# Residual added in the thirteenth pair, first pair copied to the sum; first products of the last four experts, then their second products

## The chip, the cores and the metric

The kernel runs on one core of a Trainium2 chip. The metric is the device time of one execution in microseconds (us), the median of several runs. TensorE is called PE here, VectorE DVE, ScalarE ACT, GpSimd POOL, SyncE SP; PEld is the loading of PE's stationary operand. A matrix product writes PSUM, which has eight banks.

## The reference

One decoder layer: attention over 256 tokens of width 2048, a residual and a layer norm, then a mixture of 32 experts in 4 groups, and another residual and layer norm. The change lies in the second half:

```python
def hierarchical_moe(x, w_grp, b_grp, w_rt, b_rt, w_gate, w_up, w_down):
    ...                       # one group per token, in it the two best experts: comb
    for g in range(N_GROUPS):
        h = jax.nn.silu(jnp.einsum('td,edf->tef', xt, w_gate[g])) * jnp.einsum('td,edf->tef', xt, w_up[g])
        h = h * comb[:, g, :, None]
        y = y + jnp.einsum('tef,efd->td', h, w_down[g])
    return y.reshape(B, S, D)

def reference(...):
        ...
        x = layer_norm(DEEPNORM_ALPHA * x + y, mix_ln_g[i], mix_ln_b[i])
        y = hierarchical_moe(x, ...)
        x = layer_norm(DEEPNORM_ALPHA * x + y, ffn_ln_g[i], ffn_ln_b[i])
```

Each expert has 12 MiB of weights in float32: gate and up (2048 x 512 each) and down (512 x 2048).

## The kernel before

The first 420 us are attention and the first norm. Then the 32 experts follow in 16 pairs. The tokens chosen by an expert (up to 64 in the first pass) are gathered by products with one-hot matrices, so that a pair fills the 128 rows of PE's output.

For a pair `p` the order on PE is written out by hand (`manual_schedule` for PE and SP; DVE, ACT and POOL run in program order too from the first norm on):

- **First products** (`gate_up`, L518): for each of the two experts (`side`) four blocks `j` of gate and up weights, 1 MiB each. After a block, `used` frees its two slots.
- Between the blocks of the first expert, `rest(j)` scatters a quarter of the previous pair's result back to its tokens (`scatter`, L540 and L541, tile `cb`), and DVE adds it to the sum `acc` (L548).
- `slots_of` (tile `m`) after the first expert, `hidden` after each: ACT's SiLU (L522) and DVE's multiplication (L523) give `hs`.
- The **gather** for the next pair (`pg`, L485, copied to `xg` by DVE L492 and ACT L494), eight steps through two PSUM banks that `mb()` hands out in turn; after the sixth the hidden values are transposed (`hp`, L528; `ht`, L530).
- **Second products** (`y`, L686): four steps `k` of down weights, two blocks of 1 MiB each; then ACT and DVE split the first two quarters of `y` in two parts (L534, L535, `ys_all`) for the scatter.

`residual(n)` sets the sum up, quarter by quarter in the blocks of the first expert of pair 1: PE spreads a part of the first norm's gain and shift over the 128 rows (`rows_of`, L555, tiles `g` and `b`, through `mb()`), DVE multiplies the normalised input by the gain into `acc` (L565) and adds the shift (L567). Pair 14 has eight more such broadcasts (tile `r`) for the last norm's gain and shift (copied by ACT, L667).

After pair 10 all four `rest` run in one piece, and then `further_passes`, a loop whose number of passes is read at run time (L591).

The last pair's down weights come in five column blocks (`wl`, 1 MiB each for the first three of each expert; the last two half as wide), so that `last_down` (L720), `last_add` and the sums of the last norm work block by block.

All weights come through the SP queue (L384) into a ring of slots of 1 MiB, in the order of the list `pieces`; a load is issued when a slot is free. The first 21 blocks lie ready when the experts begin.

Of the kernel before, what the change touches and what calls it, by code (L numbers as in the profile page):

```python
# [17 lines left out]
P = 128  # L18
# [11 lines left out]
LOOP_AFTER = 10  # L30
LOOP_SLOTS = 4
# [23 lines left out]
def hybrid_kernel(ctx: ExitStack, tc: tile.TileContext, x, w_qkv, w_o, ln1_g, ln1_b, w_grp, b_grp,  # L55
# [310 lines left out]
    for pr in range(NP):  # L366
# [5 lines left out]
        if pr < NP - 1:  # L372
            for k in range(4):
                pieces += [(("d", e, k), [wd_v[e, k]]) for e in (2 * pr, 2 * pr + 1)]
# [168 lines left out]
    def add_rows(name, n, ot, ys, banks, rows=P):  # L543
        for tt in range(NT):
            cb = bank(banks[tt], [P, 512], f"cb{name}_{n}_{tt}")
            scatter(cb, ot, ys, tt, rows=rows)
            t = acc[tt][:, n * 512:(n + 1) * 512]
            nc.vector.tensor_add(t, t, cb)  # L548
# [10 lines left out]
    def residual(n):  # L559

        cs = slice(n * 512, (n + 1) * 512)
        g_ = rows_of(0, n, mb(), f"g1_{n}")
        b_ = rows_of(1, n, mb(), f"b1_{n}")
        for tt in range(NT):
            nc.vector.scalar_tensor_tensor(acc[tt][:, cs].rearrange("p (a c) -> p a c", c=4), xn[tt][:, n].rearrange("p c a -> p a c"),  # L565
                                           ALPHA, g_.rearrange("p (a c) -> p a c", c=4), op0=ALU.mult, op1=ALU.mult)
# [78 lines left out]
    for p in range(NP):  # L645
# [3 lines left out]
        for side in range(2):  # L649
            e = 2 * p + side  # L650
            for j in range(4):
                gate_up(gu[side], side, lambda c: xg[:, c, side], j, held["g", e, j], held["u", e, j])
                used(("g", e, j), ("u", e, j), keep=keep)
                if p == side == 0 and j < 2:
                    for c2 in (2 * j + 4, 2 * j + 5):
                        gather(c2, xg, o2, 0)
                if p == side == 0 and j == 1:
                    gatef = gates()
                    count_passes()
                if p == 1 and side == 0:  # L660
                    residual(j)
                if side == 0 and rest is not None:
                    rest(j)
                if p == NP - 2:
                    vec = 2 + j % 2
                    n = 2 * side + j // 2
                    nc.scalar.copy(held["v", vec, 0][:, n * 512:(n + 1) * 512], rows_of(vec, n, mb(), f"r2_{n}_{vec}"))  # L667
# [4 lines left out]
        if p + 1 < NP:  # L672
            o2 = o2_next
            xg = slot(S_XG, [P, NCH, 2, CAP], f"xg{p + 1}")
            for c2 in range(8):
                gather(c2, xg, o2, p + 1)
                if c2 == 5:
                    ht = transpose_hidden(hs, p)
        else:
            ht = transpose_hidden(hs, p)  # L680
            break
        y = [bank(yb[n], [P, 512], f"y{p}_{n}") for n in range(4)]
        for k in range(4):
# [4 lines left out]
            used(("d", 2 * p, k), ("d", 2 * p + 1, k), keep=keep)  # L688
# [11 lines left out]
        if p == LOOP_AFTER:  # L700
# [4 lines left out]
            advance()  # L705

# [124 lines left out]
```

## Time and profile before

| what | value |
|---|---|
| median of 3 runs | 1395.65 us (1393.35 to 1395.83) |
| the profiled execution | 1393.51 us, its span 1391.8 us |
| busy share of the span | PE 96%, DVE 33%, ACT 24%, POOL 1% |
| granted clock of PE, mean | 0.989 |
| read from memory | 472.20 MB |
| chain of waits, by engine | PE 60%, DMA 28%, DVE 3%, ACT 2%, issue 6% |

The span goes from the first to the last instruction of the profiled execution; the rest of its time lies around it. The chain of waits is followed back from the last instruction to whatever released each step. PE counts as busy also where it runs at half clock.

### The profile page before, as it was taken

The numbers are of one execution on the slowest core, as the hardware profiler recorded it, in microseconds if no ns is written. First come the engines' busy times: TensorE is split into PE (matmuls) and PEld (weight loads), VectorE is DVE, ScalarE is ACT, GpSimd is POOL, SyncE is SP. The second block draws the span as 40 slices with busy tenths as digits, with TensorE's granted clock in tenths as the row PEclk, the third lists the DMA queues.
The fourth block names the chain that finished last, engine by engine and source line by source line (L and its number), as shares of the span: only waits on it lengthen the run. The fifth ranks groups of instructions, "written<-read, shape, count | busy, mean of one in ns | idle before, by whom it ended". The sixth has DMA issues, their size and how long they took to land.

```text
span 1391.8 us, 17936 instructions
## 1 busy us (share of the span) xinstructions
PE 1339.9 (96%) x7537; PEld 802.0 (58%) x7537; DVE 452.5 (33%) x797; ACT 332.1 (24%) x567; POOL 16.3 (1%) x39
## 2 busy tenths in 40 slices
PE   9999999999999999999999999999998999999994
PEld 8999898988895454434344344453434344344432
DVE  5454645455443151221222212212123021212116
ACT  4454535345334101101011011110101011011103
POOL 0000100000000000000000000000000000000002
PEclk9999999999999999999999999999999999999997
DMA  9745455576559889999999999999999999999993
GB/s 341 243 152 182 151 175 189 180 258 238 174 208 371 357 336 381 420 420 418 420 420 419 420 418 420 420 418 420 419 420 420 417 419 420 419 420 421 419 396 105
DMA packets 103016, 475.52 MB, mean 342 GB/s; under 512 B 12756, under 2 KB 18964, under 8 KB 54804
## 3 DMA queue, kind: packets, MB, share of 16 engines
q1 hardware_dynamic: 102932, 474.33, 86.1%
q8 instruction: 61, 1.00, 0.3%
q14 instruction: 23, 0.19, 0.0%
HBM read 472.20 MB, written 2.10 MB: 341 GB/s over the span
## 4 chain that ended last, share of the span: by engine, by line
PE 60%; DMA 28%; issue 6%; DVE 3%; ACT 2%; POOL 0%; SPq 0%; DVEq 0%; POOLq 0%; ACTq 0%
DMA wu<-in_moe_w_up_dram 20%; PE gu L518 18%; PE y L686 9%; DMA wd<-in_moe_w_down_dram 7%; PE pg L485 5%; PE pj L163 5%; PE pj L161 5%; PE pj L162 5%; PE wo L163 2%; PE wo L161 2%; PE wo L162 2%; PE cb L540 1%; PE cb L541 1%; PE y L720 1%; ACT xg L494 1%
## 5 line engine op out<-in xcount | busy, mean ns | idle before, releaser
L518 PE MATMUL gu<-wu,xg 128*64 128x512 f32 x1024 | 461.6, 600 | 7.5 <-DMA wu<-in_moe_w_up_dram 7.5
L518 PE MATMUL gu<-wg,xg 128*64 128x512 f32 x1024 | 461.1, 600 | 4.9 <-PEq L591 4.9
L518 PEld LDWEIGHTS gu<-wg,xg 128*64 128x64 f32 x1024 | 135.1, 138 | 225.7 <-issue 216.7
L686 PE MATMUL y<-wd,ht 128*64 128x512 f32 x960 | 209.3, 594 | 0.0
L518 PEld LDWEIGHTS gu<-wu,xg 128*64 128x64 f32 x1024 | 135.0, 138 | 61.7 <-issue 44.9
L161 PE MATMUL pj<-xh,ws 128*128 128x256 f32 x512 | 146.4, 286 | 0.8 <-ACT ws L151 0.8
L152 DVE TENSOR_TENSOR ws<-w,ws 128x1024 fp32r<-128x1024 f32 x88 | 107.9, 1226 | 120.7 <-ACT ws L151 120.7
L163 PE MATMUL pj<-xh,ws 128*128 128x256 f32 x512 | 146.0, 285 | 0.6 <-DVE ws L152 0.6
L162 PE MATMUL pj<-xl,ws 128*128 128x256 f32 x512 | 146.1, 286 | 0.0
L686 PEld LDWEIGHTS y<-wd,ht 128*64 128x64 f32 x960 | 67.6, 137 | 130.3 <-issue 127.6
L485 PE MATMUL pg<-o,xn 128*128 128x128 f32 x1024 | 131.5, 283 | 10.9 <-ACT xg L494 6.4
L485 PEld LDWEIGHTS pg<-o,xn 128*128 128x128 f32 x1024 | 120.3, 191 | 32.5 <-issue 13.0
L548 DVE TENSOR_TENSOR acc<-acc,cb 128x512 f32<-128x512 f32 x120 | 77.2, 684 | 181.6 <-PE cb L541 181.6
L151 ACT CAST ws<-w 128x1024 fp32r<-128x1024 f32 x88 | 92.4, 1050 | 133.6 <-PE pj L163 130.9
L534 ACT CAST ys_all<-y 128x512 fp32r<-128x512 f32 x60 | 35.1, 585 | 302.7 <-PE y L686 161.8
L535 DVE TENSOR_TENSOR ys_all<-y,ys_all 128x512 fp32r<-128x512 f32 x60 | 41.3, 688 | 184.0 <-ACT ys_all L534 181.8
L163 PEld LDWEIGHTS pj<-xh,ws 128*128 128x128 f32 x512 | 98.1, 192 | 1.3 <-DVE ws L152 1.2
L161 PEld LDWEIGHTS pj<-xh,ws 128*128 128x128 f32 x512 | 98.1, 192 | 1.2 <-ACT ws L151 1.0
L162 PEld LDWEIGHTS pj<-xl,ws 128*128 128x128 f32 x512 | 98.1, 192 | 0.1
L523 DVE SCALAR_TENSOR_TENSOR hs<-hs,gs,gu 64x512 f32<-64x512 f32 x32 | 23.9, 747 | 225.4 <-ACT hs L522 224.2
L494 ACT ACTIVATE xg<-pg,gbp 128x128 f32<-128x128 f32 x128 | 51.6, 453 | 97.7 <-PE pg L485 97.7
L492 DVE TENSOR_SCALAR xg<-pg,gbp 128x128 f32<-128x128 f32 x128 | 46.6, 406 | 85.4 <-PE pg L485 85.2
(197 smaller groups left out, 1222.4 us busy)
## 6 DMA issues: line engine op xcount, KB each, us to landing
wg<-in_moe_w_gate_dram SPq DMA_DIRECT2D x128, 1024.0 KB, 19.9
wu<-in_moe_w_up_dram SPq DMA_DIRECT2D x128, 1024.0 KB, 19.9
wd<-in_moe_w_down_dram SPq DMA_DIRECT2D x120, 1024.0 KB, 19.9
w<-in_attn_w_qkv_dram SPq DMA_DIRECT2D x44, 1024.0 KB, 5.2
wow<-in_attn_w_o_dram SPq DMA_DIRECT2D x16, 1024.0 KB, 5.1
wl<-in_moe_w_down_dram SPq DMA_DIRECT2D x6, 1024.0 KB, 17.2
wfirst<-in_attn_w_qkv_dram SPq DMA_DIRECT2D x3, 1024.0 KB, 11.0
xs<-in_x_dram SPq DMA_DIRECT2D x8, 256.0 KB, 8.3
```

Of the source, the lines that this page charges most:

```text
L151: nc.scalar.copy(t[:, 0, c], src[:, c])
L152: nc.vector.tensor_sub(t[:, 1, c], src[:, c], t[:, 0, c].bitcast(F32))
L161: nc.tensor.matmul(dst, ah, bh, start=start, stop=False, **kw)
L162: nc.tensor.matmul(dst, ah, bl, start=False, stop=False, **kw)
L163: nc.tensor.matmul(dst, al, bh, start=False, stop=stop, **kw)
L485: nc.tensor.matmul(pg[:, cc], xn[tt][:, n, c, :], o2[:, tt].rearrange("p e s -> p (e s)"), start=tt == 0, stop=tt == 1)
L492: nc.vector.tensor_scalar(to, pg[:, cc], g_, b_, op0=ALU.mult, op1=ALU.add)
L494: nc.scalar.activation(to, pg[:, cc], AF.Identity, scale=g_, bias=b_)
L518: nc.tensor.matmul(gu[to], xg(4 * j + c), w[:, c, :], start=st, stop=sp, skip_group_check=True)
L535: nc.vector.tensor_sub(ys[0:rows, 1, 0:width], y[0:rows, 0:width], ys[0:rows, 0, 0:width].bitcast(F32))
L548: nc.vector.tensor_add(t, t, cb)
L686: nc.tensor.matmul(y[n][sides[side]], ht[:, k, sides[side]], held["d", 2 * p + side, k][:, n * 512:(n + 1) * 512], start=k == 0, stop=k == ...
```

## The change

The residual moves from the first expert of pair 1 to the second expert of pair 12 (`RES_AT`, counted from 0), one quarter after each of its blocks. Since the sum is no longer set up first, pair 0's scatter is copied to `acc` instead of added. The residual is added to what the sum holds by then: the gain is spread once for each half of the tokens, multiplied in its PSUM bank by the normalised input, and added; then the shift is spread and added to both halves.

The last two pairs go in another order: first products of pair 14, first products of pair 15, second products of pair 14, its scatters in one piece, then the last products of pair 15. The list of loads follows. The banks and slots of the last stage change places accordingly.

```diff
+RES_AT = 12
...
-        if pr < NP - 1:
-            for k in range(4):
-                pieces += [(("d", e, k), [wd_v[e, k]]) for e in (2 * pr, 2 * pr + 1)]
+        if pr == NP - 1:
+            pr -= 1
+        elif pr == NP - 2:
+            continue
+        for k in range(4):
+            pieces += [(("d", e, k), [wd_v[e, k]]) for e in (2 * pr, 2 * pr + 1)]
...
-            nc.vector.tensor_add(t, t, cb)
+            if name == 0:
+                nc.vector.tensor_copy(t, cb)
+            else:
+                nc.vector.tensor_add(t, t, cb)
...
     def residual(n):
 
         cs = slice(n * 512, (n + 1) * 512)
-        g_ = rows_of(0, n, mb(), f"g1_{n}")
+        for tt in range(NT):
+            g_ = rows_of(0, n, mb(), f"g1_{n}_{tt}")
+            g4 = g_.rearrange("p (a c) -> p a c", c=4)
+            nc.vector.scalar_tensor_tensor(g4, xn[tt][:, n].rearrange("p c a -> p a c"), ALPHA, g4, op0=ALU.mult, op1=ALU.mult)
+            nc.vector.tensor_add(acc[tt][:, cs], acc[tt][:, cs], g_)
         b_ = rows_of(1, n, mb(), f"b1_{n}")
         for tt in range(NT):
-            nc.vector.scalar_tensor_tensor(acc[tt][:, cs].rearrange("p (a c) -> p a c", c=4), xn[tt][:, n].rearrange("p c a -> p a c"),
-                                           ALPHA, g_.rearrange("p (a c) -> p a c", c=4), op0=ALU.mult, op1=ALU.mult)
             nc.vector.tensor_add(acc[tt][:, cs], acc[tt][:, cs], b_)
...
+    def between(p, i):
...
+        if i < 4 and rest is not None:
+            rest(i)
+        if p == RES_AT and i >= 4:
+            residual(i - 4)
+        if p == NP - 2:
+            n, vec = divmod(i, 2)
+            nc.scalar.copy(held["v", 2 + vec, 0][:, n * 512:(n + 1) * 512], rows_of(2 + vec, n, mb(), f"r2_{n}_{vec}"))
+
+    for p in range(NP - 1):
+        hs, ot, o2 = first_products(p)
+        xg = slot(S_XG, [P, NCH, 2, CAP], f"xg{p + 1}")
+        for c2 in range(8):
+            gather(c2, xg, o2, p + 1)
+            if c2 == 5:
+                ht = transpose_hidden(hs, p)
+        if p == NP - 2:
+            rest = None
+            hs, last_ot, _ = first_products(p + 1)
+        y = second_products(p, ht)
...
+    p, ot = NP - 1, last_ot
+    ht = transpose_hidden(hs, p)
+    for n in range(4):
+        rest(n)
...
-    last_y, last_cob, lys = Rot([4, 5]), Rot([6, 7, 0, 1]), []
+    last_y, last_cob, lys = Rot([0, 1]), Rot([4, 5, 6, 7]), []
...
-        ys = slot((*S_XN, S_XG, S_YS)[n % 4], [P, 2, 512], f"ys{p}_{n}", F32R)
+        ys = slot((*S_XN, S_XG)[n % 3], [P, 2, 512], f"ys{p}_{n}", F32R)
```

`first_products`, `second_products` and `between` hold what stood in the loop's body.

On PE, this is the end of the first block of pair 1 before the change (`gu_0` is the first expert's product, `g_0` and `b_0` the broadcasts, `cb` the scatter of pair 0):

```order
3054 L518 MATMUL gu_0_4285<-wg_0_4039,xg_4168 64x512
3055 L518 MATMUL gu_0_4285<-wu_0_4087,xg_4168 64x512
3056 L555 MATMUL g_0_4300<-gb_896,ident 128x128 x4
3057 L555 MATMUL b_0_4305<-gb_896,ident 128x128 x4
3058 L540 MATMUL cb_0_0_4314<-ys_all,ot_4111 128x512
```

The broadcasts `g` and `b` are gone from there. In the changed kernel PE has them in pair 12, after each block of the second expert (`gu_1`); this is the end of the first and the beginning of the second block:

```order
4827 L522 MATMUL gu_1_7522<-wg_0_7395,xg_7401 64x512
4828 L522 MATMUL gu_1_7522<-wu_0_7397,xg_7401 64x512
4829 L562 MATMUL g_0_0_7635<-gb_896,ident 128x128 x4
4830 L562 MATMUL g_0_1_7642<-gb_896,ident 128x128 x4
4831 L562 MATMUL b_0_7649<-gb_896,ident 128x128 x4
4832 L522 MATMUL gu_1_7522<-wg_1_7477,xg_7401 64x512
```

Three broadcasts stand in a row there. On DVE, the last quarter of the residual in pair 12 of the changed kernel (`hs` is the second expert's hidden values, `xg` the gathered rows of pair 13):

```order
628 L572 SCALAR_TENSOR_TENSOR g_3_0_7734<-xn_3898,g_3_0_7734 128x512
629 L573 TENSOR_TENSOR acc_4279<-acc_4279,g_3_0_7734 128x512
630 L572 SCALAR_TENSOR_TENSOR g_3_1_7741<-xn_3899,g_3_1_7741 128x512
631 L573 TENSOR_TENSOR acc_4280<-acc_4280,g_3_1_7741 128x512
632 L576 TENSOR_TENSOR acc_4279<-acc_4279,b_3_7748 128x512
633 L576 TENSOR_TENSOR acc_4280<-acc_4280,b_3_7748 128x512
634 L527 SCALAR_TENSOR_TENSOR hs_7523<-hs_7523,gs_7617,gu_1_7522 64x512
635 L496 TENSOR_SCALAR xg_7757<-pg_0_7758,gbp 128x128 x2
```

Before, `hs` of pair 12 followed the first expert's `hs` at once. At the end, the transposition of pair 15's hidden values stood on PE right behind its first products:

```order
5308 L518 MATMUL gu_1_8440<-wg_3_8431,xg_8319 64x512
5309 L518 MATMUL gu_1_8440<-wu_3_8433,xg_8319 64x512
5310 L528 MATMUL hp_8574<-ident,hs_8441 128x128 x4
5311 L720 MATMUL y_0_8581<-wl_0_8450,ht_8579 64x512
5312 L720 MATMUL y_0_8581<-wl_1_8452,ht_8579 64x512
```

Now it stands behind pair 14's second products, and pair 14's sixteen scatter products stand between it and the last products:

```order
5296 L677 MATMUL y_3_8529<-wd_3_8458,ht_8395 64x512
5297 L677 MATMUL y_3_8529<-wd_3_8460,ht_8395 64x512
5298 L532 MATMUL hp_8566<-ident,hs_8413 128x128 x4
5299 L544 MATMUL cb_0_0_8573<-ys_all,ot_8266 128x512
5300 L545 MATMUL cb_0_0_8573<-ys_all,ot_8266 128x512
```

## Rows read from the trace of the kernel before

**Rows 1.** From the page: the rate of all transfers in 40 equal slices of the span (34.8 us each), and one group of DVE instructions (line, engine, operation, out<-in, count | busy us, mean ns | idle before and its end).

```profile
GB/s 341 243 152 182 151 175 189 180 258 238 174 208 371 357 336 381 420 420 418 420 420 419 420 418 420 420 418 420 419 420 420 417 419 420 419 420 421 419 396 105
...
L548 DVE TENSOR_TENSOR acc<-acc,cb 128x512 f32<-128x512 f32 x120 | 77.2, 684 | 181.6 <-PE cb L541 181.6
```

**Rows 2.** The chain of waits from 400 us to the end, in order of time: start us, length us, what.

```profile
469.83 13.88 PE y L686 x64
...
512.40 15.14 PE gu L518 x64
...
536.80 13.88 PE y L686 x64
...
569.93 13.93 PE gu L518 x64
583.89 0.60 ACT hs L522
...
586.06 4.12 PE pg L485 x32
...
593.12 13.88 PE y L686 x64
...
649.43 13.88 PE y L686 x64
...
780.04 19.87 DMA wu<-in_moe_w_up_dram
...
1044.68 0.60 ACT hs L522
...
1235.05 13.88 PE y L686 x64
...
1253.50 1.08 PE r L555 x8
...
1315.10 3.43 PE gu L518 x16
1319.66 3.58 PE gu L518 x16
```

**Rows 3.** What PE waited for from 1080 to 1180 us (total us, times, longest), and from PE's timeline the second products of pair 12.

```profile
PE gu L518 <- PEq L591: 4.9, 1, 4.9
PE pg L485 <- ACT xg L494: 0.8, 2, 0.4
PE pg L485 <- DVE xg L492: 0.5, 2, 0.3
...
1176.19 13.95 PE L686 MATMUL y<-wd,ht 128*64 128x512 f32 x64
```

**Rows 4.** Stretches of the span: length, then busy us (and count) of PE, PEld, DVE, ACT and POOL, PE's granted clock, the DMA share, GB/s.

```profile
480.00:560.00 80.00, 78.42 (x406) 37.36 (x404) 29.62 (x48) 9.59 (x20) 0.00 (x0) 0.98 0.90 363
560.00:780.00 220.00, 217.39 (x1107) 97.09 (x1108) 48.71 (x101) 29.56 (x63) 0.00 (x0) 1.00 1.01 419
```

**Rows 5.** Timelines of PE (first two rows and the last) and of DVE in pair 1: start us, length us, engine, line, operation, out<-in, shape, count [idle before and what ended it].

```profile
486.55 0.59 PE L518 MATMUL gu<-wg,xg 128*64 128x512 f32 x1
487.07 1.15 PE L555 MATMUL g<-gb,ident 16*128 16x128 f32 x8
...
488.26 1.03 DVE L565 SCALAR_TENSOR_TENSOR acc<-xn,g 128x512 f32<-128x512 f32 x1 [4.91 <-PE g L555]
489.40 0.69 DVE L567 TENSOR_TENSOR acc<-acc,b 128x512 f32<-128x512 f32 x1
490.00 1.06 DVE L565 SCALAR_TENSOR_TENSOR acc<-xn,g 128x512 f32<-128x512 f32 x1
...
510.06 1.02 DVE L565 SCALAR_TENSOR_TENSOR acc<-xn,g 128x512 f32<-128x512 f32 x1
...
511.23 0.52 PE L503 MATMUL m<-ident,o 128*128 128x128 f32 x2 [0.92 <-DVE acc L565]
```

**Rows 6.** Short stretches, with the columns of rows 4: behind the last quarter of the residual in pair 1, and among the scatters of pair 10.

```profile
512.00:513.00 1.00, 1.00 (x4) 0.61 (x6) 1.00 (x3) 0.54 (x2) 0.00 (x0) 0.50 0.93 393
...
1072.00:1074.00 2.00, 1.49 (x5) 0.79 (x6) 1.71 (x4) 0.00 (x0) 0.00 (x0) 1.00 1.03 426
```

**Rows 7.** PE's timeline at the scatters of pair 10, with the columns of rows 5.

```profile
1067.73 0.50 PE L540 MATMUL cb<-ys_all,ot 128*128 128x512 f32 x1
...
1072.33 0.47 PE L540 MATMUL cb<-ys_all,ot 128*128 128x512 f32 x1 [1.15 <-DVE ys_all L535]
...
1074.14 0.40 PE L541 MATMUL cb<-ys_all,ot 128*128 128x512 f32 x1
```

**Rows 8.** PE's timeline at the last products, with the columns of rows 5.

```profile
1349.70 0.66 PE L528 MATMUL hp<-ident,hs 128*128 128x128 f32 x4 [1.48 <-DVE hs L523]
1351.04 8.78 PE L720 MATMUL y<-wl,ht 128*64 128x512 f32 x32 [0.68 <-ACT ht L530]
...
1360.87 3.65 PE L720 MATMUL y<-wl,ht 128*64 128x512 f32 x16
...
1368.58 1.95 PE L720 MATMUL y<-wl,ht 128*64 128x256 f32 x16
```

**Rows 9.** What reads or loads the tile `wl`: the issues of its loads (duration ns min/median/max, first and last start us), and the us from issue to landing.

```profile
L384 SPq DMA_DIRECT2D wl<-in_moe_w_down_dram x10: 373/2508/9307, 1324.8 to 1354.7; - x10
...
DMA to landing us min/median/max: 9.6/13.6/20.3
```

More of the change, by code (lines that the diff above doesn't have):

```diff
@@ L644, in hybrid_kernel, with first_products @@
     gatef, ys_all, acc, rest = None, None, None, None
-    for p in range(NP):
+    def first_products(p):
         keep = LOOP_SLOTS if p == LOOP_AFTER else 0
@@ L653, in hybrid_kernel @@
                 used(("g", e, j), ("u", e, j), keep=keep)
[L654 to L667, printed above, removed]
+                between(p, 4 * side + j)
             if side == 0:
@@ L671, in hybrid_kernel, with second_products @@
             hidden(gu[side], side, gs, hs)
[L672 to L681, printed above, removed]
+        return hs, ot, o2_next
+    def second_products(p, ht):
         y = [bank(yb[n], [P, 512], f"y{p}_{n}") for n in range(4)]
@@ L687, in hybrid_kernel @@
                                      start=k == 0, stop=k == 3, skip_group_check=True)
-            used(("d", 2 * p, k), ("d", 2 * p + 1, k), keep=keep)
+            used(("d", 2 * p, k), ("d", 2 * p + 1, k), keep=LOOP_SLOTS if p == LOOP_AFTER else 0)
+        return y
+    def between(p, i):
+        nonlocal gatef
+        if p == 0 and i < 2:
+            for c2 in (2 * i + 4, 2 * i + 5):
+                gather(c2, xg, o2, 0)
+        if p == 0 and i == 1:
+            gatef = gates()
+            count_passes()
+        if i < 4 and rest is not None:
[16 more added lines that the diff above has]
+        y = second_products(p, ht)
         if p == 0:
```

## The prediction, made before the changed kernel was run

> **What bounds the kernel now.** I read the page first, then the chain of waits from 400 us on. The loads move 417 to 421 GB/s from the seventeenth slice almost to the end, and TensorE (PE) is busy 96% of the span, so a busy share decides nothing [rows 1]. A pair of experts loads 24 blocks of 1 MiB, 25.2 MB, which at 420 GB/s takes 59.9 us. PE alone needs 56.3 us for a pair: that is the distance between the second products of pairs 1, 2 and 3 (536.80, 593.12, 649.43) [rows 2]. The two are close, and the chain shows who holds when:
>
> - Until 780 us PE holds. Pair 1, with the residual in it, takes 66.97 us (469.83 to 536.80), 10.66 more than the others [rows 2].
> - From 780 us the loads hold, up to the first products of pair 10, which end at 1044.68 on a late load [rows 2].
> - Pair 10 runs its four scatters in one piece and then reaches the branch of the further passes, where PE stands 4.9 us. Between 1080 and 1180 us PE waits for no load at all, only 1.3 us inside gathers [rows 3]. The loads have caught up with it in pair 13 alone: second products start at 1176.19 and 1235.05, 58.86 us apart, so PE waited 2.55 us there [rows 2, 3].
> - From there to the final block the chain is PE again, and pair 14 carries eight row broadcasts for the last norm on top [rows 2]. The last weight load is issued at 1354.7 and lands at least 9.6 us later, 1364.3 [rows 9]; the products that use it start at 1368.58 [rows 8]. PE, not the loads, sets the end, with some 4 us of margin.
>
> So work taken from pair 1 is worth what it lets the loads do before 560 us, and work put into pair 12 stands in a stretch where PE is the late one.
>
> **Step 1, the residual leaves pair 1.** PE is up to 10.66 us earlier from pair 2 on. In time this counts only as far as the loads come forward, since they hold between 780 and 1044 us. From 480 to 560 us they moved 363 GB/s, against 419 from 560 to 780 us [rows 4]. The shortfall is 80 x (1 - 363/420) = 10.9 us of load time. PE cannot give back more than 10.66, and a little of the shortfall lies ahead of the first quarter at 487. With PE releasing slots as in pairs 2 to 5, where the rate is full, I take **-10.2 us**. Bounds: nothing (the idle moves elsewhere), and 10.66.
> Copying pair 0 instead of adding replaces eight 684 ns additions on VectorE (DVE), which is 37% busy there [rows 4]: nothing, and at twice the price 5.5 us in 56, still covered.
>
> **Step 2, the waiting of pair 13.** If PE arrives later there, its 2.55 us of waiting vanish first: **-2.55 us**.
>
> **Step 3, the residual in pair 12.** It stands between the blocks of the second expert, and asks three broadcasts for each quarter (gain twice, shift once) through two PSUM banks. So the third broadcast waits until DVE has multiplied and added the first. From the rows of pair 1, counted from the first broadcast's start: the multiplication starts at 1.19 (487.07, 488.26), the addition 1.14 later (489.40), lasts 0.69, so the bank is free at 3.02 [rows 5]. PE follows DVE by about 0.15 (the last multiplication began at 510.06, lasts 1.02, and PE went on at 511.23): the third broadcast starts at 3.17. The next first product comes 1.08 later, at 4.25. Without all this it would come 0.09 before the start, as pairs of first products follow each other at 13.93 / 32 = 0.43 [rows 2] and the broadcast came 0.52 after the last one (486.55) [rows 5]. Each of the first three quarters costs 4.34 us, 13.0 together.
>
> The last quarter is followed by no block but by the hidden values. The DVE order puts their multiplication behind the residual's six operations: two pairs of 1.74, two additions at 0.60 steps, so it starts 5.87 after the first broadcast. Now PE's third gather starts 2.17 after the activation of the hidden values (583.89, 586.06), and 1.55 of that follows the activation's 0.60 and the hand-over [rows 2]. The third gather then comes at 5.87 + 1.55 = 7.42, where it came at 2.27 on the same scale. That is 5.15 us more. Step 3 costs **+18.2 us**. No row shows a multiplication that writes PSUM; I use the 1.03 us of the one that writes SBUF, it enters the first three quarters once and the last twice. With 0.68, the addition's price [rows 1], the step is 1.75 less; with half as much again, 1.55, it is 2.6 more. Lower bound 10.66, what it cost in pair 1 without the bank waits.
>
> The clock adds to this. In pair 1 the clock held through three quarters (0.98 on the mean from 480 to 560 us leaves room for 3.2 us at half [rows 4]) and fell to 0.50 (1.2 GHz) after the fourth, where PE did two broadcasts, four scatters and then stood 0.92 us; the 64 products behind it took 15.14 us instead of 13.93, 1.2 more [rows 2, 5, 6]. The new quarters have three broadcasts, no scatter, and a hole of about 1 us each. I take two falls in four, **+2.4 us**; bounds 0 and 4 x 1.48 = 5.9, with the dearer fall of [rows 8].
> The Trainium skill (TensorE: Matmul & The Clock Gate, "What's actually happening") says that half rate is the default and that only activity lifts the gate; by that, taken strictly, every one of the four thin stretches falls back. By it the sum is that of the rival below in which every quarter drops the clock. The row of the fourth quarter agrees [rows 6], the three before it do not [rows 4].
>
> **Step 4, the order of the last four experts.** The loads keep their bytes; only second weights of pair 14 and first weights of pair 15 change places, and with the loads 10 us early nothing in it is waited for. PE loses the scatters between the first products of pair 15, four times 1.14 = 4.56 us (1315.10 to 1319.66 holds 4.56 where the products alone take 3.43) [rows 2]. It also loses the hole in which the last hidden values were made, 1.48 + 0.66 + 0.68 = 2.82 us; second products now cover it [rows 8]. It gains one transposition (0.66) and pair 14's scatters in one piece: at pair 10 these run from 1067.73 to 1074.54, 6.8 us [rows 7]. Net 7.46 - 4.56 - 2.82 = **+0.1 us**. The clock fell in the old hole: 32 records took 8.78 us, two times 3.65 would be 7.30, so 1.48 went there [rows 8]. At pair 10 the clock held through the scatters' own hole of 1.15 us [rows 6, 7]; I credit half, **-0.7 us**; bounds 0 and -1.48.
>
> **Sum.** -10.2 - 2.55 + 18.2 + 2.4 + 0.1 - 0.7 = +7.25 us. The profiled execution took 1393.51 us (span 1391.8 and 1.7 around it), which is 2.1 under the median of the runs; 1393.5 + 7.25 = 1400.75. I say 1401.
>
> **Rivals.**
> - *Faster: the block costs in pair 12 only what it did in pair 1.* Step 3 with its clock is then 10.66, the sum -10.2 - 2.55 + 10.66 + 0.1 - 0.7 = -2.7, 1390.8 us. For it: DVE was only 37% busy even around pair 1 [rows 4], and two of the three broadcasts are the old ones. Against: three broadcasts on two banks cannot avoid DVE. The sign turns where step 3 costs 13.35 us.
> - *The loads cover pair 12.* If PE waited for the loads all through pairs 11 and 12, as it does in pair 10, the block would lie in that waiting and the end would move with the loads, 10.2 us earlier: 1383. Against: no wait for a load from 1080 to 1180 [rows 3].
> The Trainium skill (DMA: Bandwidth & Descriptors, "Specifications") gives 358 GB/s of HBM per core; by that a pair would load in 70.3 us (an estimate), and PE would wait nearly everywhere. The trace has 420 GB/s [rows 1], and that decides.
> - *Every quarter drops the clock.* 18.2 + 5.9 - 12.75 + 0.1 = +11.45, 1405 us.
> - *The loads do not come forward.* Then PE still waits for them up to 1044 us, and the sum is 7.25 + 10.2 = +17.45: 1411 us. Against: with pairs of 56.3 us the same ring keeps the loads full from 560 us on [rows 2, 4].
>
> **How the numbers follow.** Forecast 0.57, all quarters slow 0.16, block as cheap as in pair 1 0.13, covered 0.06, loads not forward 0.05, shortfalls that cancel 0.03. The measurement tells 0.2%, 2.8 us, from no change. The cheap block lies on that edge, half on each side; the low part of the forecast (about 0.07) is within it. Faster 0.06 + 0.06 = 0.12, same 0.07 + 0.03 + 0.07 = 0.17, slower 0.71. The range runs from the cheap block to above the slow quarters: 1390.5 to 1408; outside lie the covered and the not-forward case, 0.11, and some scatter.
>
> **What would show it.** Pair 1 should take 56.3 us and the loads be full from 490 us. First products of pair 10 should end near 1034.5. Pair 12 should take 74 to 80 us, with holes of 1 us before each third broadcast that end on DVE. Pair 13 should show no wait for a load. From the end of pair 15's first products to the first of the last products should lie 13.9 + 7.5 us. The last load should land near 1354, 15 us or more ahead of its use. I am wrong if pair 12 takes under 70 us, or if pair 10 is not earlier.

## The result, and the profile of the changed kernel

The changed kernel takes 1409.95 us (median of 4 runs, 1405.19 to 1411.15); the kernel before took 1394.62 beside it. The ratio is 1.0109, with a 95% interval of 1.0093 to 1.0126: slower, as forecast, but by 15 us and not by 7, and outside the range of 1390.5 to 1408.

The profiled execution is the fastest of the four, 1405.19 us with a span of 1403.5, 11.7 more than the span before. It is read first; what the others have more of comes out of the experiments.

**The loads and pair 1.** The page's row of the rate of all transfers, in 40 equal slices (35.1 us each), against [rows 1]:

```profile
GB/s 342 238 151 182 148 173 188 180 263 240 178 196 384 359 419 419 420 418 420 420 419 420 420 418 420 419 420 420 420 418 419 419 419 417 390 406 419 347 324 60
```

The loads are full from the fifteenth slice (491 us) on, where they had two slices at 336 and 381. They are full up to 1190 us and then dip in some slices: at the end the loads are ahead and wait for room (behind 1160 us the SP queue waits 93.6 us for first products to free their slots).

**The branch behind pair 10.** The first row is where pair 10's first products end and its gathers begin (PE's timeline; 1044.65 before). Then the last scatter, and the first product behind the branch, which came at 1079.44 before:

```profile
1036.23 2.05 PE L489 MATMUL pg<-o,xn 128*128 128x128 f32 x16
...
1065.80 0.40 PE L545 MATMUL cb<-ys_all,ot 128*128 128x512 f32 x1
1076.42 1.09 PE L522 MATMUL gu<-wg,xg 128*64 128x512 f32 x1 [10.23 <-PEq L600]
```

PE is 8.4 us earlier into the gathers and only 3.0 earlier out of the branch. The stand, PE's idle time at the branch, has grown from 4.9 us [rows 3] to 10.2. What the branch's line holds tells where (engine queue, operation, count: ns min/median/max, first and last start), first of the kernel before, then of the changed one:

```profile
L591 PEldq COMPARE_BRANCH  x2: 101/206/310, 1078.0 to 1078.2; - x2
```

```profile
L600 DVEq COMPARE_BRANCH  x2: 51/56/61, 1069.6 to 1069.7; - x2
L600 PEldq COMPARE_BRANCH  x2: 101/2996/5890, 1069.7 to 1069.8; - x2
```

The other engines branch in 0.06 us in both. PE's longer one takes 5.89 us where it took 0.31, and all engines wait for it: on each of them the last semaphore of this line starts at 1076.3 us.

**Pair 12.** The chain of waits (start us, length us, what), from the second products of pair 11 to those of pair 13; the answers to [rows 5] stand in it:

```profile
1115.78 13.88 PE y L677 x64
...
1152.52 1.10 PE g L562 x8
...
1153.64 1.04 DVE g L572
...
1154.71 0.70 DVE acc L573
...
1155.54 1.12 PE b L562 x8
1156.66 3.58 PE gu L522 x16
...
1163.26 1.12 PE b L562 x8
1164.38 5.28 PE gu L522 x16
...
1172.68 1.12 PE b L562 x8
1173.80 3.58 PE gu L522 x16
...
1192.68 7.44 PE y L677 x33
...
1249.00 13.88 PE y L677 x64
```

What PE waited for before each third broadcast, from 1080 us to the end (total us, times, longest):

```profile
PE b L562 <- DVE acc L573: 4.1, 4, 1.0
```

Pair 12 takes 76.90 us (1115.78 to 1192.68), 20.6 over the 56.3 of a plain pair. A quarter is seen in the first rows: a broadcast, then DVE multiplies (1.04) and adds (0.70), then the third broadcast, and the next block 4.14 us after the quarter began. The four holes, short idle times of PE before the third broadcast, are 1.0 us each and end on DVE's addition. Of the blocks behind the first three quarters one takes 5.28 us in place of 3.58: the granted clock has fallen there (0.64 from 1164 to 1167 us), and it falls again behind the fourth quarter (0.59 from 1182 to 1186). These are the two falls of this execution. Pair 13 takes 56.32 (1192.68 to 1249.00): it no longer waits for loads.

**The end.** PE's timeline, against [rows 8]:

```profile
1357.33 0.66 PE L532 MATMUL hp<-ident,hs 128*128 128x128 f32 x4
...
1364.46 7.09 PE L745 MATMUL y<-wl,ht 128*64 128x512 f32 x32
1372.60 3.65 PE L745 MATMUL y<-wl,ht 128*64 128x512 f32 x16
```

The 32 records of the last products take 7.09 us (8.78 before). From the second products of pair 13 to the third block of last products it is 123.60 us (1249.00 to 1372.60), where it was 125.82 (1235.05 to 1360.87, [rows 2, 8]).

So the 11.7 us of the profiled execution are: -8.4 into the gathers of pair 10, +5.4 at the branch, -1.1 from there to the second products of pair 11 (PE is at half clock for a shorter time behind the stand: 0.50, 0.73 and 1.00 granted in its first three stretches of 2 us, where it was 0.50, 0.50 and 0.64), +20.6 in pair 12, -2.55 in pair 13, -2.2 at the end.

### The profile page after: what moved, and what is told of

It reads as the page before. It is cut to its first block, busy times and chain, and to the rows that moved or that the text cites. A ratio compares the mean times of both kernels' runs of the same rounds, so it can differ in the third digit from the quotient of the medians.

```text
span 1403.5 us, 18006 instructions
## 1 busy us (share of the span) xinstructions
PE 1343.9 (96%) x7569; PEld 805.7 (57%) x7569; DVE 457.4 (33%) x805; ACT 332.3 (24%) x567; POOL 16.3 (1%) x39
## 5 line engine op out<-in xcount | busy, mean ns | idle before, releaser
L522 PE MATMUL gu<-wg,xg 128*64 128x512 f32 x1024 | 459.9, 599 | 10.2 <-PEq L600 10.2
L555 DVE TENSOR_TENSOR acc<-acc,cb 128x512 f32<-128x512 f32 x112 | 72.1, 684 | 169.8 <-PE cb L545 169.8
```

The costliest lines, as they stand in the source:

```text
L522: nc.tensor.matmul(gu[to], xg(4 * j + c), w[:, c, :], start=st, stop=sp, skip_group_check=True)
```

## The experiments

Each kernel ran beside the kernel before, whose medians lay between 1393.3 and 1394.9 us; a difference of 2 us between kernels that did not run side by side says little. "The changed kernel" takes 1410 to 1411.

### The changed kernel again

No edit. 

> The changed kernel, unchanged, for a second profile. The first profile shows 1405.2 us: a longer stand at the branch behind pair 10 (10.2 us on TensorE, 4.9 before) takes 5.3 us, and pair 12 takes 76.9 us with two falls of the clock. The other runs of the same kernel take 1410 us, some 5 us more. Theory A: in a usual run all four quarters of the residual drop the clock; then pair 12 takes 79 to 80 us here and the stand is again about 10 us. Theory B: the stand at the branch differs from run to run; then it is 13 to 15 us here, pair 12 about 77. Theory C: neither, the 5 us lie elsewhere (the start, or half clock in other pairs); then both stretches are as in the first profile at a time near 1410. Should this profile also come out at 1405, nothing is decided by it.

Measured: median 1410.8 us (6 runs, 1403.6 to 1412.3), ratio 1.0119 (1.0102 to 1.0136); the profiled run is again the fastest, 1403.6. It starts its experts as early as the kernel before, and its first products of pair 10 end here:

```profile
1034.41 2.05 PE L489 MATMUL pg<-o,xn 128*128 128x128 f32 x16
```

That is the 1034.5 of the forecast; the 1.8 us by which the first profile is later lie in its start. Pair 12 takes 76.91 us with falls in the same two places, and PE's branch takes 6.15 us. On the slower runs these two profiles decide nothing, as the expectation said for this case. But each run has its mean granted clock on record: of these six the fastest has 0.987, the next (1406.6) 0.985, and the four above 1410 have 0.981 to 0.983. So the slower ones spend more time at half clock; where, the next profiles show for two kernels near to this one.

### The residual moved, the last four experts in the old order

```diff
-        if pr == NP - 1:
-            pr -= 1
-        elif pr == NP - 2:
-            continue
...
-        if p == NP - 2:
-            rest = None
-            hs, last_ot, _ = first_products(p + 1)
...
```

> The changed kernel with the last four experts in the order of the kernel before: the residual alone is moved. Theory: the new order at the end is worth 2.2 us (123.6 us from the second products of pair 13 to the third last block, 125.8 before), so about 1412 us, pair 12 and the stand at the branch as in the changed kernel (77 and 10 us). Rival: the new order at the end is what costs; then 1400 us or less, near the forecast of 1401 or below it.

Measured: 1408.91 us (1406.17 to 1414.02), ratio 1.0095 (1.0075 to 1.0115). The rival falls: the new order is not the loss. The profiled run takes 1414.02 us. Its stretches at pair 12's second expert (length, busy us and count of PE, PEld, DVE, ACT, POOL, PE's granted clock, DMA share, GB/s):

```profile
1150.00:1155.00 5.00, 5.00 (x30) 2.46 (x30) 1.95 (x7) 0.97 (x2) 0.00 (x0) 1.00 1.01 418
1156.00:1160.00 4.00, 3.27 (x12) 2.11 (x14) 3.50 (x5) 0.00 (x0) 0.00 (x0) 0.62 1.01 420
1168.00:1172.00 4.00, 4.00 (x14) 2.29 (x16) 2.54 (x4) 0.00 (x0) 0.00 (x0) 0.50 1.01 420
1180.00:1184.00 4.00, 4.00 (x14) 1.26 (x12) 1.23 (x3) 0.00 (x0) 0.00 (x0) 0.61 1.01 420
1188.00:1192.00 4.00, 4.00 (x18) 3.77 (x19) 3.37 (x5) 0.00 (x0) 0.00 (x0) 0.50 0.99 412
```

The clock is whole when the residual begins and falls to one half (1.2 GHz) behind each of the four quarters. Pair 12 takes 83.95 us here (second products at 1116.97 and 1200.92), 7.05 more than in the two profiles with two falls. This is theory A of the first expectation, at a higher price than it gave (79 to 80). The end takes 124.2 us in the old order, with 7.09 us for the 32 records of the last products:

```profile
1373.27 7.09 PE L738 MATMUL y<-wl,ht 128*64 128x512 f32 x32 [0.67 <-ACT ht L531]
1381.42 3.65 PE L738 MATMUL y<-wl,ht 128*64 128x512 f32 x16
```

So of the 2.2 us at the end 1.6 belong to a fall of the clock that the old order had in the profile of the kernel before and not in this one; the order itself is worth 0.6 here.

### The new order at the end alone

```diff
...
+        if p == 1 and i < 4:
+            residual(i)
...
-        if p == RES_AT and i >= 4:
-            residual(i - 4)
```

`residual` and the addition of pair 0's scatter are those of the kernel before.

> The kernel before with the new order of the last four experts alone: the residual stays in pair 1. Theory: the end gains about 2.2 us and nothing else moves; 1392 to 1393 us, the stand at the branch 4.9 us as in the kernel before, since no instruction ahead of it has changed. Rival one: the new order costs; 1396 us or more. Rival two: the longer stand at the branch comes from what lies behind it in the program (the end is written differently); then the stand is near 10 us here too, and the time 1397 or so.

Measured: 1396.13 us, ratio 1.0020 (1.0009 to 1.0031). My theory, a gain of 2 us, falls. Rival two falls too: PE's branch takes 0.40 us and the stand is 3.0. What PE waited for from 1080 us to the end (total us, times, longest):

```profile
PE gu L522 <- DMA wu<-in_moe_w_up_dram: 2.3, 2, 1.3
PE y L672 <- DMA wd<-in_moe_w_down_dram: 2.0, 1, 2.0
```

With the residual in pair 1 the loads are late to the end, and the new order has PE wait 2.0 us for second weights of pair 14. Rival one holds in its number, by 1.3 us. That this wait makes the 1.3 us is argued: the ten runs spread over 6.9 us, and in this profile pair 13's second products, which come ahead of everything that was reordered, are already 1.7 us later than in the profile before.

### One broadcast of the gain for a quarter

```diff
-        for tt in range(NT):
-            g_ = rows_of(0, n, mb(), f"g1_{n}_{tt}")
...
-            nc.vector.tensor_add(acc[tt][:, cs], acc[tt][:, cs], g_)
+        g_ = rows_of(0, n, mb(), f"g1_{n}")
         b_ = rows_of(1, n, mb(), f"b1_{n}")
+        for tt in range(NT):
+            gx = bank(yb[2 * (n % 2) + tt], [P, 512], f"gx{n}_{tt}")
...
+            nc.vector.tensor_add(acc[tt][:, cs], acc[tt][:, cs], gx)
```

> The changed kernel, with one row broadcast of the gain for a quarter in place of two, and the products written to free PSUM banks: the third broadcast and the wait for its bank are gone, the six operations of VectorE for a quarter stay. Theory: a quarter then costs TensorE two broadcasts, about 2.2 us, in place of 4.34, so pair 12 takes 6 us less (about 70 us), and with no hole of 1 us the clock falls only behind the last quarter, 1 to 3 us more: 1400 to 1404 us. Rival: the broadcasts and the bank wait are not what costs, VectorE's chain is (the hidden multiplication behind six operations, and the additions late); then pair 12 falls by 2 us or less and the time is 1407 or more.

Measured: 1397.25 us (10 runs within 1395.76 to 1397.94), ratio 1.0015 (1.0005 to 1.0024): 13 us less than the changed kernel. The chain in its pair 12:

```profile
1153.27 1.08 PE g L562 x8
1154.36 0.89 PE b L562 x8
1155.25 3.58 PE gu L522 x16
...
1160.81 3.58 PE gu L522 x16
...
1166.37 3.58 PE gu L522 x16
```

Each of the first three quarters costs 1.98 us, no block behind one takes more than 3.58, and pair 12 takes 67.97 us (1116.57 to 1184.54). Behind the fourth, where PE waits 2.0 us for DVE, the clock falls here too (0.50 from 1174 to 1176 us). The theory holds and gave too little (1400 to 1404): 8.9 us against the profile with two falls, 16 against the run with four. That all its runs lie within 2.2 us, where the changed kernel's spread over 8.7, fits a spread made by the number of falls, but does not show it: the kernel before, with two broadcasts in a row, spread over 5.4 us in 19 runs beside this one.

### Three broadcasts without the wait for a bank

```diff
+    rb = Rot([4, 5, 6, 7])
...
+        g_ = [rows_of(0, n, rb(), f"g1_{n}_{tt}") for tt in range(NT)]
+        b_ = rows_of(1, n, rb(), f"b1_{n}")
...
-            g_ = rows_of(0, n, mb(), f"g1_{n}_{tt}")
...
-        b_ = rows_of(1, n, mb(), f"b1_{n}")
```

> The changed kernel with all three row broadcasts of a quarter in PSUM banks that are free at that time; only the wait of the third broadcast for its bank is gone, its products and VectorE's operations stay. A usual run of the changed residual shows four falls of the clock (pair 12 takes 84 us, 7 more than in the profile with two falls). Theory: the holes of 1 us let the clock fall; without them the first three quarters cost three broadcasts each, 3.2 us in place of 4.34, and hold the clock, so pair 12 takes 72 to 74 us and the kernel about 1399 us. Rival: the row broadcasts themselves, 24 thin products in a row, let the clock fall; then the holes alone are gone, pair 12 is 79 us or more, and the kernel takes 1406 to 1408.

Measured: 1403.54 us (1400.34 to 1404.30), ratio 1.0070 (1.0052 to 1.0087): 6 to 7 less than the changed kernel. The chain in pair 12:

```profile
1150.61 1.98 PE g L562 x16
1152.59 0.89 PE b L562 x8
1153.48 3.58 PE gu L522 x16
...
1160.34 6.50 PE gu L522 x16
...
1169.71 5.24 PE gu L522 x16
...
1182.27 5.48 PE pg L489 x32
```

The three broadcasts now run without a hole, in 2.87 us for 4.14, and the clock still falls behind the second, third and fourth quarter (32 gathers behind the fourth take 5.48 us, 4.12 at whole clock). Pair 12 takes 76.78 us. Neither expectation is met whole: the holes are not what makes the clock fall, the rival is right in that; but the wait was worth 1.3 us in each of the first three quarters (4.14 less 2.87), and one fall less than four the rest. In these kernels three broadcasts of 16 rows in a row lose the clock mostly, with or without a hole, and two did not in any of the first three quarters.

### The length of the program ahead of the branch

```diff
+        if p == 8 and i >= 4:
+            keep_warm(16, mb(), zero)
```

The loop of `keep_warm` issues 16 products of zeros each time, 64 in all; the second kernel has 32 in its place, 128 in all.

> The changed kernel with 64 products whose result nobody reads in pair 8, which puts TensorE's program ahead of the branch back to the length that it has in the kernel before. PE waits for loads there, so the products themselves cost little. Theory: the stand of 10.2 us at the branch (5.9 to 6.2 us of it in TensorE's compare-and-branch, 0.3 in the kernel before) comes from where the instructions behind the loop lie relative to those in front of it; with the old length the branch takes 0.3 to 0.4 us again, the stand is 3 to 5 us, and the kernel is 5 us faster than the changed one: 1405 usually. Rival: the stand comes from the earlier arrival or from what follows the branch; then it stays at 10 us and the time at 1410.

> The same with 128 products in place of 64. Theory: what counts is the place within a block of instructions that is loaded as one; 128 products are 256 instructions (a weight load and a product each), as much as the 16 KB that one instruction packet of the trace carries, if an instruction takes 64 bytes. So the place within the block is that of the changed kernel, and the long branch of 5.9 to 6.2 us comes back. Rival: a longer program ahead of the branch helps in itself; then the branch takes 0.3 us as with 64.

Measured: 1408.06 us with 64 products (ratio 1.0109, 1.0092 to 1.0125), 1410.23 with 128 (one run). The branch's line of each, 64 first:

```profile
L600 PEldq COMPARE_BRANCH  x2: 97/204/310, 1069.4 to 1069.5; - x2
```

```profile
L600 PEldq COMPARE_BRANCH  x2: 97/3094/6090, 1068.0 to 1068.1; - x2
```

64 products bring back the 0.31 us of the kernel before, and the stand is 5.0 us; 128 bring back 6.09 and 10.5. The rivals fall: neither the earlier arrival, nor what follows, nor a longer program as such decides, but the length of the program ahead, and 256 instructions more give what none give. The change took 64 records of PE and as many weight loads out of pair 1, 128 instructions, and put none back ahead of the branch.

The traces hold the fetch itself. They have 61 instruction packets (queue q8) of 1.00 MB in all, 16 KB each, and in every profile one of them begins behind the branch. In the changed kernel PE's branch runs from 1069.8 to 1075.7 us and the packet from 1073.2 to 1074.2; in all profiles with a long branch the branch ends 1.4 to 1.5 us behind the packet. Where the branch is short a packet also begins, 3.5 to 3.7 us behind the branch, and PE is long past by then. So the long branch waits for a block of instructions, which costs 5.6 to 5.8 us. The Trainium skill (Runtime: NRT & Kernel Launch, "Instruction fetch mechanics") says that instructions are fetched in blocks of 256, and that a taken branch whose target lies outside the blocks at hand waits for a fetch. These traces agree, with the packets of 16 KB and the return of the long branch at 256 instructions more.

In the time the shorter branch is not clear of the spread. The kernel with 64 products takes 1408.06 us, 2 to 3 less than the changed one and not 5, and its ratio to the kernel beside it is the same 1.0109. What its profile shows is the stretch that holds the branch: from the second products of pair 10 to those of pair 11 it is 65.67 us, where it was 70.21. Pair 12 gives most of that back with three falls (79.97 us in a run of 1403.41), and the three other runs have the granted clock of the changed kernel's slowest, 0.981. What the unread products themselves cost in pair 8 was not measured apart.

The changed kernel was profiled only in its two shortest executions, with two falls each. The kernel with 128 products shows what I take for a usual one, 1410.23 us, with these rows in pair 12's chain:

```profile
1154.39 2.04 PE b L562 x8
1156.44 5.64 PE gu L522 x16
...
1166.22 5.28 PE gu L522 x16
...
1176.56 5.82 PE gu L522 x16
...
1197.61 8.73 PE y L677 x39
```

All four quarters lose the clock here. In the first and the third quarter the last broadcast takes 2.04 us for 1.12, and the blocks behind the first three take 5.64, 5.28 and 5.82 for 3.58; the 48 gathers behind the fourth take 7.62 for 6.17, nearly as in the first profile (7.67). That is 0.92 + 2.06 + 1.70 + 0.92 + 2.24 + 1.45 = 9.3 us. Pair 12 takes 82.98 us (from 1114.63), 6.1 more than in the fastest runs. That and 1405.2 make 1411, about what the others take; that those had four falls too is argued from this, from the run of 1414.02 above and from their mean clock.

### The residual in pair 8

```diff
-RES_AT = 12
+RES_AT = 8
```

> The changed kernel with the residual in pair 8 in place of pair 12, one number changed. Theory: from 780 to 1044 us the loads hold and PE waits, so some of the residual's 20 to 28 us lies in that waiting (6 us of waits are shown, and the loads' lead grows while PE is late, to be used up behind it); behind the branch nothing is added. The branch lies 192 instructions further on and should be short. Time: 1410 less 20 to 28 less 5, plus what PE can't catch up by pair 10, some 5 to 12 us: 1382 to 1395, faster than the kernel before. Rival: PE is as late at the end as it is behind pair 8, since it needs 56.3 us of the loads' 59.9 for a pair and gains only 3.6 us a pair; then the residual costs its whole 20 us less 9: 1398 or more.

Measured: 1396.17 us (10 runs), ratio 1.0017 (1.0008 to 1.0027): 14 less than the changed kernel, and no gain on the one before. Between the two expectations: PE waits for no load at all between 560 us and the end, so the residual used up that waiting and the rest stayed. In the changed kernel pairs 8 to 10 take 10.5 us more than three plain pairs; here pair 8 takes 82.92 and the two behind it 56.32 each, so that of its 26.6 us over a plain pair 16.1 remain. Some 4 of the 14 us come from the shorter stand, 6.3 us where it was 10.2. The clock fell there too:

```profile
880.00:920.00 40.00, 37.92 (x176) 17.48 (x174) 16.87 (x27) 2.14 (x4) 0.00 (x0) 0.90 1.01 420
920.00:960.00 40.00, 37.01 (x194) 21.94 (x192) 12.82 (x21) 4.30 (x10) 0.00 (x0) 0.85 1.00 412
```

PE's branch takes 4.03 us: 192 instructions further on than in the changed kernel it is neither short nor at its longest. That I had expected short. It too ends 1.5 us behind its instruction packet, but the packet begins 1.5 us after the branch and not 3.3 to 3.7 as in the other profiles.

### The changed kernel without the residual

```diff
-        if p == RES_AT and i >= 4:
-            residual(i - 4)
```

> The changed kernel without the residual: this part of the computation is left out, its gain, shift and additions. The difference to the changed kernel is what pair 12 pays for it. Theory: 1410.5 less the 27 to 28 us by which pair 12 exceeds 56.3 us in a usual run: 1383, with the long branch still in it (10 us, the program ahead of the branch has the length of the changed kernel's). Rival: the loads hold as soon as pair 12 is short (they are full at 419 GB/s from 490 us on); then 1388 or more, and the residual costs less than its stretch.

Measured: 1385.44 us (1384.58 to 1386.61), ratio 0.9938 (0.9921 to 0.9955), with a branch of 6.15 us and no wait for a load behind 1080 us. The residual in pair 12 costs the changed kernel 25 us in the median. The time lies halfway between theory (1383) and rival (1388); the rival's reason, loads that hold behind the short pair 12, is not met, as PE waits for none there.

### Two broadcasts in pair 8; one broadcast for a block; that with the old end

```diff
-RES_AT = 12
+RES_AT = 8
...
-        if p == RES_AT and i >= 4:
-            residual(i - 4)
+        if p == RES_AT and 3 <= i < 7:
+            gain(i - 3)
+        if p == RES_AT + 1 and 3 <= i < 7:
+            shift(i - 3)
```

All three have the one broadcast of the gain from above, and `RES_AT = 8`. The first keeps `residual` as one block; the second and third split it into `gain`, the first broadcast with its two multiplications and two additions, and `shift`, the other broadcast with its two additions. The third has the old order of the last experts as well.

> The residual in pair 8 with one broadcast of the gain for a quarter, its products in free banks (the two edits that gained before, together). In pair 8 alone PE waited for no load at all behind 560 us any more, and was the bound all through; with two broadcasts the residual takes 11.7 us in place of 20 to 28, about what PE waited for loads in the changed kernel (10 us). Theory: second products of pair 10 where the changed kernel has them, the branch 0.3 us (the program ahead has the length of the kernel before), nothing in pair 12: 1376 to 1384 us. Rival: the clock falls in pair 8 as it did there with three broadcasts (granted 0.85 to 0.90 from 880 to 960 us), and the time is 1388 or more.

> As that, with one broadcast behind a block of first products: the gain of the four quarters in pair 8, the shift in pair 9, each behind the fourth to the seventh of a pair's eight blocks, so that the last block is followed by the hidden values as without a residual. Theory: what lets the clock fall is the length of the thin stretch between two blocks, 2 us and more; one broadcast of 1.08 us does not (as in pair 14, which holds its clock with one for each block), the last quarter's wait of 3.7 us is gone too, and eight broadcasts cost 8 us in all: as fast as the two broadcasts in pair 8 or up to 5 us faster, 1374 to 1382 us; no stretch of pairs 8 and 9 below a granted clock of 0.98. Rival: the loads hold from pair 8 to the end in both; then the two are the same within 1 us.

> The spread residual with the last four experts in the old order. Where PE is the bound at the end, the new order is worth 0.6 to 2.2 us (123.6 us from the second products of pair 13 to the third last block, 124.3 and 125.9 in the old order). Theory: this is 1 to 2 us slower than the spread residual with the new order. Rival: the loads hold at the end here, and the new order asks for the first weights of the last two experts earlier and for second weights as late as before; then the two are the same, or the old order is faster by 1 to 3 us, as the new order alone was no gain on the kernel before.

Measured: 1385.25 us for two broadcasts in pair 8, 1385.60 for the spread residual, and 1383.36 (1382.43 to 1383.50) for the spread residual with the old end; ratios 0.9939 (0.9922 to 0.9956), 0.9940 (0.9924 to 0.9957) and 0.9921 (0.9904 to 0.9938). All three beat both kernels, and the last, with the residual moved and the order of the last experts left alone, is the best. The branch takes 0.31 to 0.42 us in all three, at the program length of the kernel before, and the stand 2.9 to 5.0, so that 5 to 7 of the 25 us by which they beat the changed kernel come from there. With two broadcasts pair 8 takes 69.11 us and the clock falls only behind the fourth quarter (1.00 from 880 to 920 us, 0.91 from 920 to 960).

The spread residual holds its clock: from 880 to 1040 us it is granted whole.

```profile
880.00:1040.00 160.00, 158.46 (x810) 72.76 (x806) 54.19 (x96) 19.53 (x41) 0.00 (x0) 1.00 1.01 419
```

Yet it is no faster than two broadcasts in pair 8, and the two with the new end stay above what I expected (1376 to 1384 and 1374 to 1382). The second rival is right in that they are the same within 1 us, since the loads hold in both in pair 13 (59.94 and 59.25 us, 56.32 without a wait) and at the end (2.2 us of waits for second weights); in pairs 9 and 10 of the first kernel PE holds, 56.36 and 56.31 us. For the third the rival is right too, that the old order is faster by 1 to 3 us. The chain of the spread residual with the new end, at its end:

```profile
1313.47 19.91 DMA wd<-in_moe_w_down_dram
1333.43 3.65 PE y L682 x14
...
1344.21 7.02 PE y L752 x32
```

and with the old end:

```profile
1325.75 13.91 PE gu L519 x64
...
1342.44 7.09 PE y L745 x32
```

In the new order the last load that PE waits for is one of second weights of pair 14, and behind it stand a piece of those products, sixteen scatter products and their holes: 10.8 us until the last products (1333.43 to 1344.21). In the old order no load is waited for behind pair 13, and 2.8 us lie between the end of the last first products and the last products (1339.66 to 1342.44). So where the loads are the late ones at the end the new order costs 2.2 us, and where PE is, as in the changed kernel, it gains 0.6 by the profiles.

## Why the prediction was wrong, step by step

**Step 1 (-10.2 us)** was right. Pair 1 takes 56.35 us, the loads are full from 491 us, and pair 10's first products end at 1034.4 in the second profile, 10.3 earlier.

**A step that is missing: the branch.** I took the stand at the branch as a fixed 4.9 us that moves along with pair 10. It grew by 5.3, because the change altered how many instructions stand ahead of it. No row of before was long there. But the branch was in the chain, the change took 128 instructions from in front of it, and what it costs to fetch the target where that falls badly was a term with an unknown price, which should have been in the range. Half of what step 1 gave was lost here. The two kernels with unread products and the instruction packets show the cause of the stand; that the 5.3 us reach the end is read from the chain, since the times of the two kernels do not resolve it.

**Step 2 (-2.55 us)** was right: pair 13 takes 56.32.

**Step 3, the blocks (+18.2 us)** was right in its mechanism and 0.8 too high. A quarter takes 4.14 us from its first broadcast to the next block (4.25 reckoned), the holes of 1.04 end on DVE, and in the profile with two falls the 20.6 us hold 1.7 for the one and 1.5 for the other (48 gathers in 7.67 us for 6.17, which is 4.12 for 32 and 2.05 for 16 at whole clock), which leaves 17.4. The open price, a multiplication that writes PSUM, measured 1.04 us against the 1.03 that I used.

**Step 3, the clock (+2.4 us)** is the term that was mis-sized. Two falls of four were taken at 1.2 us each. The usual execution, as far as the profiles of two kernels near to it and the mean clock of the runs tell, has four, and pair 12 is then 83.0 us: 26.7 over a plain pair, less 17.4, so 9.3 us for the clock, which is also the sum of its rows above. Even my upper bound, 5.9, was too low, because its price for a fall (1.48) came from a place where PE had no thin products at half clock; here the broadcast behind the hole is lengthened as well (0.92), and the block by 1.7 to 2.2. The case that every quarter drops the clock, to which I gave 0.16, was the usual one in number: four of four at 0.50 to 0.62 in the run with the old end. In both profiles of the changed kernel two of the four held. The Trainium skill (TensorE: Matmul & The Clock Gate, "What's actually happening") says that the throttled state is the default and that activity releases it. Taken strictly, as in the prediction, that asks for a fall in every quarter; the traces agree in some executions and not in others.

**Step 4 (+0.1 and -0.7 us)** came out at -2.2 in the profile: -0.6 for the order and -1.6 for the fall. In the chain of the changed kernel it is that small because PE is the bound there; the condition that I gave, loads 10 us early, is what it hangs on. The 1.6 us are luck of the execution in which the kernel before was profiled. The last load is issued at 1355.0 us and lands 9.7 to 15.5 us later, not near 1354 as I had it; its products start at 1380.3, so the margin is 10 to 15.6 us, where I had 15 or more. From the end of pair 15's first products to the last products it is 21.0 us, 21.4 reckoned.

**The sum.** With -10.2, -2.55, 17.4, the end at -2.2 and -1.1 behind the branch it is +1.4; the branch's 5.3 and the clock's 9.3 make it 16.0, so 1409.5 us. Measured: 1409.95. That it comes so near is in part luck, since the 2.2 and the 1.1 hold falls of the clock in single executions. Of these 16 us 9.3 are clock and 5.3 the branch; without the two the change would have been close to none.

**The rivals.** Loads covering pair 12 did not happen. The cheap block is what two broadcasts make: 11.7 us in pair 12, and 1397. "Every quarter drops the clock" (1405) was the right mechanism at too low a price, and without the branch.

## What to carry to other kernels

Price a thin stretch on TensorE together with what the clock does behind it, from rows in which thin products themselves ran at half clock, and take all of the stretches as falling when the bound is sought; here one broadcast fewer without the wait was worth 13 us, moving the work to where PE waits for loads 14, and both together 25 (4 to 7 of these last two are the shorter branch), while single broadcasts behind full blocks held the clock and saved no further time. When a loop or branch stands in the chain, count the instructions that a change adds or removes ahead of it, and allow for a fetch of instructions at its end. An order at the end of a kernel is good or bad by who is late there: the same edit gained 0.6 us with PE late and cost 2.2 with the loads late.

## What the runs showed of the hardware that was not expected

- A taken branch of TensorE over a loop that is not entered takes 0.31 to 0.42 us or 5.9 to 6.15, by the place of the program: 0.31 with 128 instructions more ahead of it than in the changed kernel, 6.09 with 256 more, and 4.03 with 192 more. In each long case it ends 1.4 to 1.5 us behind a packet of 16 KB of instructions. Why that packet begins 2 us sooner with 192 is open.
- The same 24 products of 16 rows, three broadcasts, lost the clock behind two, three or four of the four quarters in profiles of the changed kernel and of kernels near to it. The changed kernel's times spread over 8.7 us, with the mean granted clock at 0.987 in the fastest of six runs and at 0.981 in the slowest; the four kernels with one or two broadcasts behind a block of pair 8 or 12 kept within 2.2 us each.
